# A hybrid encoder layer on one core: block sums taken by VectorE straight from the accumulator banks, and a later operand split issued directly behind its last product

## The chip, the core and the metric

The kernel runs on one core of a Trainium2 chip. The metric is device time in microseconds for one execution; the times before are 1273.06, 1273.35 and 1274.11 us, median 1273.35. The engines are TensorE (PE, with weight loads shown as PEld), VectorE (DVE), ScalarE (ACT), GpSimd (POOL) and SyncE (SP, which issues nearly all transfers). Each engine works through its own instructions in the order in which the program wrote them, and waits for semaphores where an operand or a buffer is not ready.

## What is computed

One layer on x of 1024 positions by 1024 channels, all in float32:

```
proj = x @ w_in + b_in                  # u | h | c_gate | b_gate | gate_a | gate_b
y_a  = S5 state space scan of u;  g = gelu(y_a)
y_a  = (g * sigmoid(g @ glu_w + glu_b)) @ w_ssm_out
y_b  = (b_gate * causal_conv(c_gate * h)) @ w_conv_out
mix  = (sigmoid(gate_a) * y_a + sigmoid(gate_b) * y_b) @ w_o
x    = layer_norm(ALPHA * x + mix)
ffn  = (silu(x @ w_gate) * (x @ w_up)) @ w_down
x    = layer_norm(ALPHA * x + ffn)
```

The gelu is the tanh form, 0.5 y (1 + tanh(c (y + 0.044715 y^3))). Below, v = b_gate * causal_conv(c_gate * h).

## The kernel before

**Tiling.** The three large products (input projection, gate and up projections of the FFN, down projection) use Strassen's seven products in place of eight. A `Pair` takes two column blocks of 128 weights; with the two halves of the inner dimension and the two halves of the 1024 positions this is a 2 by 2 block product, made of products 1 to 7 (`WOP` and `XOP` say which weight and operand blocks are added for each). A product is twelve matmuls of 128 x 512: every float32 operand is split into a rounded high part and a low remainder, and low x high, high x low and high x high are accumulated for four blocks of 128 (`Entry.mm`, L183 to L185). The high part is made by ScalarE, the low part by VectorE (`split` L120, `psplit` L131), the weight sums by GpSimd (`do_add`, L106 in `tt`).

**Sums of a pair.** The seven products of a pair go into four banks (`BANK_OF`): b0 takes products 2 then 4, b1 takes 5 then 3, b2 takes 1 then 7, b3 takes 6. b0 and b1 at their end are two of the four results. The other two need sums over banks, which `Pair.ev` issues after each product. Before the change: ScalarE copies b0 after product 2 (`ta`, L239), b1 after product 5 (`tb`, L242) and b2 after product 1 (`tc`, L245); GpSimd adds ta = ta + tb (L247, helper line L112) and tc = tc - ta (L250, helper line L115); VectorE then makes tb = b0 - ta (L265), tc = b1 + tc (L269), and adds b2 and b3 at the end (L271, L273). A bank may take its second product only when the first has been read out, and may go to another pair only when its last reader is done. Where one of the two GpSimd sums was issued in the same call, `wait` puts VectorE's part off to the call after the next product (`later`, `flush`).

**Order.** A program-wide list of steps, one per product, sets the order. At step s, `run` issues in turn: the weight sum of step s+4, the split of step s+3, one turn of every background generator (`bg`: the set-up of the scan, its eight chunks, the convolution, the gelu), the matmuls of s, what was put off, the step's `mid` functions and then `ev`. The input projection has 14 pairs, the FFN 22. In both, the first three pairs are interleaved, product by product (`LEAD_A`, `LEAD_D`; from here on the leads): 2, 4, 5, 3 for the three pairs in turn, then 1 and the rest. While they run, the operand blocks for the later products are still being made (`make_x`, `x1_rest`), and in the input projection the set-up of the scan runs on VectorE too. From the fourth pair on a pair's products follow one another: 2, 5, 1, 4, 3, 7, 6. The leads have six product banks between them; in the FFN the first two results of a pair stay in their banks until the gate is applied, and those of the third pair are copied out (`keep`, L256).

**v.** The conv branch's product with w_conv_out follows the input projection. Its operand v was written to memory and read back; `begin_b` splits it into vh and vl (eight pieces, ScalarE and VectorE), in place of the operands of the input projection. It was a `mid` function of the last step of the input projection, so behind that step's background turn and what was put off.

**gelu.** A background generator per tile of y_a: y is copied from its bank (L807), squared (L827), y (1/0.044715 + y^2) is made by VectorE (L830), ScalarE halves y in place (L831), then the tanh (L834) and the last product (L838).

Of the kernel before, what the change touches and what calls it, by code (L numbers as in the profile page):

```python
# [47 lines left out]
def kernel(  # L48
# [112 lines left out]
    class Step:  # L161
        load = add = split = mm = None

        def __init__(self):
            self.pre = []
            self.mid = []
            self.after = []

# [18 lines left out]
    class Pair:  # L187
        def __init__(self, s0, s1, nm, combos, epilogue):
# [4 lines left out]
            self.whole = {}  # L193
            self.done = set()
# [12 lines left out]
        def ev(self, m):  # L207
            d, e = self.done, self.evd
            d.add(m)
            fresh = set()  # L210

            def wait(name):
                if name in fresh:
                    later.append(lambda: self.ev(m))
                    fresh.discard(name)
                    fresh.add("-" + name)
                return "-" + name in fresh
# [22 lines left out]
            if once("cb", {5}):  # L240
                self.tb = tile("eb")
                S.activation(self.tb, self.b[1], AF.Copy)  # L242
            if once("cc", {1}):
                self.tc = tile("ec")
                S.activation(self.tc, self.b[2], AF.Copy)  # L245
            if once("s", {2, 5}):
                add(self.ta, self.ta, self.tb, G)  # L247
                fresh.add("s")
            if once("cs", {1}, "s"):
                sub(self.tc, self.tc, self.ta, G)  # L250
                fresh.add("cs")
# [10 lines left out]
            if 4 in d and "t11" not in e and wait("s"):  # L262
                pass
            elif once("t11", {4}, "s"):
                tt(self.tb, self.b[0], self.ta, ALU.subtract)  # L265
            if 3 in d and "t22" not in e and wait("cs"):
                pass
            elif once("t22", {3}, "cs"):
                add(self.tc, self.b[1], self.tc)  # L269
# [69 lines left out]

    def run(lo, hi):  # L340
        for s in range(lo, hi):
# [6 lines left out]
            for it in list(bg):  # L348
                if it[1] <= s:
                    try:  # L350
                        it[1] = s + max(1, next(it[0]) or 1)
                    except StopIteration:
                        bg.remove(it)
            steps[s].mm()
# [134 lines left out]
    for p in pairs[:3]:  # L489
        p.drops = {4: 1}  # L490
        p.whole = {2: wsum, 5: wsum}
    add_pairs(pairs, LEAD_A, 3)
# [272 lines left out]
    def flow(cc):  # L765
# [41 lines left out]
        S.activation(yn, ps, AF.Copy)  # L807
# [8 lines left out]
    def gelu(tl):  # L816
        yield 1
        for hs in ((0, 1),) if tl == 3 else ((0,), (1,)):
# [7 lines left out]
            for h in hs:  # L826
                S.activation(t[h], yf[h], AF.Square)  # L827
            yield 1
            for h in hs:
                V.scalar_tensor_tensor(t[h], t[h], 1.0 / 0.044715, yf[h], ALU.add, ALU.mult)  # L830
                S.activation(yf[h], yf[h], AF.Copy, scale=0.5)  # L831
            yield 2
            for h in hs:
                S.activation(t[h], t[h], AF.Tanh, scale=0.044715 * math.sqrt(2.0 / math.pi))  # L834
# [886 lines left out]
```

## Time and profile before

| | |
|---|---|
| median of three runs | 1273.35 us |
| the profiled execution, by its own time | 1274.3 us |
| span of the profile | 1272.5 us |
| PE busy | 1207.5 us (95% of the span) |
| DVE, ACT, POOL busy | 832.9, 764.7, 786.2 us |
| mean granted TensorE clock | 0.98 of full |

A row of a timeline gives the start, the time taken, engine, line, operation, output<-inputs, and in brackets the idle time before it and what ended that. Buffer numbers are left out of names. In names, the pair is the suffix: u (the pairs of u), hc (h with c_gate), b (b_gate), gt (gate_a with gate_b), f (FFN). `ps` is a product bank, `ea`, `eb`, `ec` are ta, tb, tc (in the second pair of a lead they are called `z`), `wh` and `wl` are high and low parts of weights, `xh`, `xl`, `x1h`, `x1l` those of operands, `hp` is a copy of the high part in a bank, `t` a weight sum, `xs` and `x1s` operand sums, `scr` the set-up of the scan.

### The profile page before, as it was taken

Reading aid. Unit: us, or ns where it says so; the run is one execution under the profiler, and the core shown is the slowest. Engines: PE = TensorE matmul, PEld = TensorE weight load, DVE = VectorE, ACT = ScalarE, POOL = GpSimd, SP = SyncE. Lnnn points to the kernel's source line nnn. Section 1 sums busy time; section 2 is a strip of 40 time slices with the busy share of each in tenths; the row PEclk is TensorE's granted clock in tenths of the full one; section 3 lists DMA queues with packets and bytes.
Section 4 is the critical chain, followed back from the end, with each engine's and each line's share of the span. In section 5 each row is a group of like instructions: output and inputs, shape, how many; then the busy total and the mean of one; then the engine's idle time right before and its main releaser. Section 6 shows DMA issues by size and latency. Waiting matters only on the chain. (4 is left out here: it accounts for less than half of the span.)

```text
span 1272.5 us, 16760 instructions
## 1 busy us (share of the span) xinstructions
PE 1207.5 (95%) x5341; PEld 977.6 (77%) x5341; DVE 832.9 (65%) x1338; ACT 764.7 (60%) x1360; POOL 786.2 (62%) x593
## 2 busy tenths in 40 slices
PE   7769999999899999999989999999999999999996
PEld 4547787787677888888867888888888887888776
DVE  6986887979665656688775444444444447667777
ACT  4676777696877333233674555554555655778891
POOL 4747787787762114323398787777787764544466
PEclk9989999999999999999989999999999999999998
DMA  7222334344447544324303522233223417937312
GB/s 262 67 68 92 86 123 119 112 130 137 136 141 228 193 158 163 113 87 143 139 34 116 181 101 108 94 113 116 98 93 108 153 71 267 370 100 214 101 47 87
DMA packets 88456, 167.63 MB, mean 132 GB/s; under 512 B 17841, under 2 KB 27057, under 8 KB 88113
## 3 DMA queue, kind: packets, MB, share of 16 engines
q1 hardware_dynamic: 87760, 166.44, 39.2%
q8 instruction: 42, 0.69, 0.2%
q14 instruction: 46, 0.37, 0.1%
q10 hardware_dynamic: 608, 0.13, 0.1%
HBM read 116.34 MB, written 44.83 MB: 127 GB/s over the span
## 5 line engine op out<-in xcount | busy, mean ns | idle before, releaser
L183 PE MATMUL ps_f<-x1h,wl_f 128*128 128x512 f32 x616 | 241.8, 393 | 6.0 <-ACT keep L256 2.3
L184 PE MATMUL ps_f<-x1l,wh_f 128*128 128x512 f32 x616 | 241.1, 391 | 1.9 <-DVE x1l L115 1.9
L185 PE MATMUL ps_f<-x1h,wh_f 128*128 128x512 f32 x616 | 240.9, 391 | 0.0
L115 DVE TENSOR_TENSOR wl_f<-t_f,hp 128x512 fp32r<-128x512 f32 x107 | 73.5, 687 | 167.9 <-ACT hp L137 167.5
L137 ACT ACTIVATE hp<-t_f 128x512 fp32r<-128x512 f32 x107 | 64.4, 601 | 163.6 <-POOL t_f L106 162.7
L183 PEld LDWEIGHTS ps_f<-x1h,wl_f 128*128 128x128 f32 x616 | 116.2, 189 | 32.2 <-ACT keep L256 2.8
L184 PEld LDWEIGHTS ps_f<-x1l,wh_f 128*128 128x128 f32 x616 | 116.5, 189 | 26.6 <-DVE x1l L115 2.3
L185 PEld LDWEIGHTS ps_f<-x1h,wh_f 128*128 128x128 f32 x616 | 116.4, 189 | 24.4
L106 POOL TENSOR_TENSOR tB<-B,B 128x512 f32<-128x512 f32 x55 | 71.2, 1294 | 85.1 <-DVE rBl L115 45.4
L1542 PE MATMUL pe<-rBh,rAl 128*128 128x512 f32 x297 | 116.1, 391 | 2.5 <-DVE acc L112 1.6
L1543 PE MATMUL pe<-rBl,rAh 128*128 128x512 f32 x297 | 115.8, 390 | 1.2 <-DVE rBl L115 1.2
L1544 PE MATMUL pe<-rBh,rAh 128*128 128x512 f32 x297 | 115.6, 389 | 0.0
L183 PE MATMUL ps_gt<-xh,wl_gt 128*128 128x512 f32 x216 | 88.9, 412 | 13.6 <-ACT ec_gt L245 3.7
L185 PE MATMUL ps_gt<-xh,wh_gt 128*128 128x512 f32 x216 | 87.1, 403 | 0.0
L184 PE MATMUL ps_gt<-xl,wh_gt 128*128 128x512 f32 x216 | 86.9, 403 | 0.0
L106 POOL TENSOR_TENSOR t_f<-raw_f,raw_f 128x512 f32<-128x512 f32 x63 | 81.8, 1300 | 2.2 <-DVE wl_f L115 2.0
L1542 PEld LDWEIGHTS pe<-rBh,rAl 128*128 128x128 f32 x297 | 55.8, 188 | 16.2 <-DVE acc L112 2.5
L1543 PEld LDWEIGHTS pe<-rBl,rAh 128*128 128x128 f32 x297 | 55.8, 188 | 13.3 <-DVE rBl L115 1.9
L138 ACT ACTIVATE wh_f<-t_f 128x512 fp32r<-128x512 f32 x107 | 66.0, 617 | 0.0
L1544 PEld LDWEIGHTS pe<-rBh,rAh 128*128 128x128 f32 x297 | 55.8, 188 | 11.6
L183 PEld LDWEIGHTS ps_gt<-xh,wl_gt 128*128 128x128 f32 x216 | 41.8, 194 | 26.6 <-ACT ec_gt L245 4.7
L109 POOL TENSOR_TENSOR hid<-sgf,ec_f 128x512 f32<-128x512 f32 x21 | 27.5, 1308 | 54.0 <-DVE sgf L109 29.1
(411 smaller groups left out, 3271.1 us busy)
## 6 DMA issues: line engine op xcount, KB each, us to landing
raw_f<-in_wgu SPq DMA_DIRECT2D x45, 512.0 KB, 4.0
As<-a_d SPq DMA_DIRECT2D x77, 256.0 KB, 3.9
a_d<-hs SPq DMA_DIRECT2D x55, 256.0 KB, 2.0
B<-in_wd SPq DMA_DIRECT2D x44, 256.0 KB, 5.4
s_d<-sg SPq DMA_DIRECT2D x32, 256.0 KB, 2.8
sgd<-s_d SPq DMA_DIRECT2D x16, 512.0 KB, 4.0
raw_gt<-in_w SPq DMA_DIRECT2D x15, 512.0 KB, 4.7
a_d<-hid SPq DMA_DIRECT2D x22, 256.0 KB, 2.1
```

Source lines behind the costliest of these rows:

```text
L106: eng.tensor_tensor(o, a, b, op)
L109: eng.tensor_tensor(o, a, b, ALU.mult)
L115: eng.tensor_tensor(o, a, b, ALU.subtract)
L137: S.activation(hp, raw, AF.Copy)
L138: S.activation(hi, raw, AF.Copy)
L183: PE.matmul(ps, self.lo[:, k, :], xh[:, k, :], start=first and k == 0, stop=False, skip_group_check=True)
L184: PE.matmul(ps, self.hi[:, k, :], xl[:, k, :], start=False, stop=False, skip_group_check=True)
L185: PE.matmul(ps, self.hi[:, k, :], xh[:, k, :], start=False, stop=last and k == 3, skip_group_check=True)
L1542: PE.matmul(ps, al[:, c], bh, start=kp == 0, stop=False)
L1543: PE.matmul(ps, ah[:, c], bl, start=False, stop=False)
L1544: PE.matmul(ps, ah[:, c], bh, start=False, stop=kp == NK - 1)
```

## The change

In `ev`, a pair that is `direct` keeps only the copy of b0. VectorE makes ta = b1 + ta from the bank behind product 5, and takes b2 and b1 straight into tc (x1 behind product 1, x3 behind product 3, whichever comes first starting tc by subtracting ta). `wait` is gone: nothing is put off but the two last epilogues. All 22 FFN pairs and the first three pairs of the input projection are direct. The eleven later pairs of the input projection keep the copies and the GpSimd sums. A pair that is `early` (the third of a lead) takes x3 only behind product 1. `begin_b` moves to directly behind the matmuls of the last step of the input projection, ahead of that step's background turn. In the gelu the factor 0.5 goes into the copy from the bank, with factors of 2 in the square and in the tanh to make up for it, and the halving goes.

```
-            if once("cb", {5}):
+            if not self.direct and once("cb", {5}):
                 self.tb = tile("eb")
                 S.activation(self.tb, self.b[1], AF.Copy)
-            if once("cc", {1}):
-                self.tc = tile("ec")
-                S.activation(self.tc, self.b[2], AF.Copy)
             if once("s", {2, 5}):
-                add(self.ta, self.ta, self.tb, G)
-                fresh.add("s")
-            if once("cs", {1}, "s"):
-                sub(self.tc, self.tc, self.ta, G)
-                fresh.add("cs")
+                if self.tb is None:
+                    tt(self.ta, self.b[1], self.ta, ALU.add)
+                else:
+                    add(self.ta, self.ta, self.tb, G)
+            banks = list(self.b)
...
-            if 4 in d and "t11" not in e and wait("s"):
-                pass
-            elif once("t11", {4}, "s"):
+            if once("t11", {4}, "s"):
+                if self.tb is None:
+                    self.tb = tile("eb")
                 tt(self.tb, self.b[0], self.ta, ALU.subtract)
-            if 3 in d and "t22" not in e and wait("cs"):
-                pass
-            elif once("t22", {3}, "cs"):
-                add(self.tc, self.b[1], self.tc)
+            for name, need, bk in (("x1", {1}, banks[2]), ("x3", {3}, banks[1])):
+                if (1 in d or not self.early) and once(name, need, "s"):
+                    if self.tc is None:
+                        self.tc = tile("ec")
+                        if self.direct:
+                            tt(self.tc, bk, self.ta, ALU.subtract)
+                        else:
+                            S.activation(self.tc, bk, AF.Copy)
+                            sub(self.tc, self.tc, self.ta, G)
+                    else:
+                        add(self.tc, bk, self.tc)
+            once("t22", set(), "x1", "x3")
...
+            if steps[s].next:
+                steps[s].mm()
+                steps[s].next()
+                advance(s)
+            else:
+                advance(s)
+                steps[s].mm()
...
+    for p in pairs[3:]:
+        p.direct = False
...
-        S.activation(yn, ps, AF.Copy)
+        S.activation(yn, ps, AF.Copy, scale=0.5)
...
-                S.activation(t[h], yf[h], AF.Square)
+                S.activation(t[h], yf[h], AF.Square, scale=2.0)
...
-                S.activation(yf[h], yf[h], AF.Copy, scale=0.5)
...
-                S.activation(t[h], t[h], AF.Tanh, scale=0.044715 * math.sqrt(2.0 / math.pi))
+                S.activation(t[h], t[h], AF.Tanh, scale=2.0 * 0.044715 * math.sqrt(2.0 / math.pi))
...
-    steps[n_co - 1].mid.append(begin_b)
+    steps[n_co - 1].next = begin_b
```

(`advance` is the loop over the background generators that stood in `run`.) In all, ScalarE loses 58 instructions (25 pairs by two copies, and eight halvings), GpSimd 50, VectorE gains 50. TensorE and SP keep their order unchanged. Three places show what moves.

The first is VectorE in the lead of the input projection, a piece of the difference, from about the third product of the first pair on (names ending in u and z_u are the first and second pair, gt the third).

```order
 L115 TENSOR_TENSOR xl_293<-xs_291,hp_346 128x512
+L106 TENSOR_TENSOR ea_u_196<-ps_u_1_337,ea_u_196 128x512
+L106 TENSOR_TENSOR eb_u_351<-ps_u_0_186,ea_u_196 128x512
 L115 TENSOR_TENSOR wl_u_3_356<-raw_u_0_198,hp_357 128x512
 L112 TENSOR_TENSOR scr<-scr 128x32 x3
 L118 TENSOR_SCALAR scr<-scr 128x32
 L115 TENSOR_TENSOR scr<-scr 128x32
-L106 TENSOR_TENSOR eb_u_350<-ps_u_0_186,ea_u_196 128x512
 L115 TENSOR_TENSOR xl_293<-xs_291,xh_292 128x512
```

The sum ta of the first pair is new on VectorE, and the subtraction behind it, which had been put off past the next split and three set-up rows, now stands directly behind it; both are ahead of the weights wl of the next product.

The second is ScalarE where the input projection ends: before,

```order
492 L121 ACTIVATE wh_so_1_0_3787<-raw_so_1_3679 128x512
493 L831 ACTIVATE gy_0_3715<-gy_0_3715 128x512
494 L831 ACTIVATE gy_1_3717<-gy_1_3717 128x512
495 L421 ACTIVATE sg_0_0_3821<-eb_gt_3704,b1s 128x512
496 L121 ACTIVATE vh<-vr_z 128x512
497 L121 ACTIVATE vh<-vr_ws 128x512
```

and now:

```order
480 L121 ACTIVATE wh_so_1_0_3775<-raw_so_1_3667 128x512
481 L121 ACTIVATE vh<-vr_z 128x512
482 L121 ACTIVATE vh<-vr_ws 128x512
483 L121 ACTIVATE vh<-vr_3549 128x512
484 L121 ACTIVATE vh<-vr_3575 128x512
```

Both halvings are gone from ahead of the first piece of vh, and the gate's sigmoid has moved behind the eighth. On VectorE nothing moves there.

The third is GpSimd in the lead of the FFN: before,

```order
237 L106 TENSOR_TENSOR x1s_0_5763<-M 128x512 x2
238 L112 TENSOR_TENSOR ea_f_5588<-ea_f_5588,eb_f_5772 128x512
239 L106 TENSOR_TENSOR x1s_2_5797<-M 128x512 x2
240 L112 TENSOR_TENSOR z_f_5613<-z_f_5613 128x512
241 L106 TENSOR_TENSOR t_f_1_5808<-raw_f_0_5394,raw_f_1_5639 128x512
242 L106 TENSOR_TENSOR x1s_0_5832<-M 128x512
243 L112 TENSOR_TENSOR ea_f_5637<-ea_f_5637,eb_f_5836 128x512
244 L106 TENSOR_TENSOR t_f_1_5839<-raw_f_0_5590,raw_f_1_5713 128x512
245 L106 TENSOR_TENSOR x1s_2_5865<-M 128x512
```

and now:

```order
231 L106 TENSOR_TENSOR x1s_0_5749<-M 128x512 x2
232 L106 TENSOR_TENSOR x1s_2_5782<-M 128x512 x2
233 L106 TENSOR_TENSOR t_f_1_5793<-raw_f_0_5380,raw_f_1_5625 128x512
234 L106 TENSOR_TENSOR x1s_0_5816<-M 128x512
235 L106 TENSOR_TENSOR t_f_1_5823<-raw_f_0_5576,raw_f_1_5699 128x512
236 L106 TENSOR_TENSOR x1s_2_5848<-M 128x512
```

The sums ta of the three pairs are gone from between the operand sums (x1s) and the weight sums (t). Three more go further on (the subtractions of tc, before at rows 251, 253 and 264).

More of the change, by code (lines that the diff above doesn't have):

```diff
@@ L167, in __init__ @@
             self.after = []
+            self.next = None
     class Entry:
@@ L193, in __init__ @@
             self.whole = {}
+            self.tb = self.tc = None
+            self.direct = True
             self.done = set()
@@ L209, in ev @@
             d.add(m)
[L210 to L217, printed above, removed]
             def once(name, need, *evs):
@@ L338, in flush, with advance @@
             f()
+    def advance(s):
+        for it in list(bg):
+            if it[1] <= s:
+                try:
+                    it[1] = s + max(1, next(it[0]) or 1)
+                except StopIteration:
+                    bg.remove(it)
     def run(lo, hi):
@@ L347, in run @@
                 steps[s + 3].split()
[L348 to L354, printed above, removed]
+            if steps[s].next:
[5 more added lines that the diff above has]
+                steps[s].mm()
             flush()
```

## The prediction

> **What bounds the kernel now.** I read the stages first, because the page's mean busy shares mix stages with different limits.
>
> ```profile
> core 0: us, PE busy (x) PEld busy (x) DVE busy (x) ACT busy (x) POOL busy (x), PEclk, DMA share, GB/s
> 46.00:100.00 54.00, 36.37 (x122) 27.16 (x121) 49.98 (x89) 35.42 (x62) 29.16 (x22) 0.82 0.18 54
> 100.00:405.00 305.00, 290.07 (x1381) 235.41 (x1381) 228.60 (x320) 225.38 (x383) 226.27 (x162) 0.99 0.43 132
> 405.00:412.00 7.00, 4.14 (x11) 2.75 (x10) 5.69 (x11) 6.17 (x12) 0.00 (x0) 0.76 0.44 130
> 646.00:696.00 50.00, 42.37 (x166) 32.79 (x166) 31.40 (x41) 28.98 (x54) 43.70 (x33) 0.93 0.20 72
> 696.00:1040.00 344.00, 344.00 (x1519) 284.82 (x1518) 149.47 (x234) 186.55 (x342) 262.48 (x210) 1.00 0.33 116
> ```
>
> Nineteen of the 22 FFN pairs lie in the last stretch, and there TensorE is busy for all of 344 us at full clock: 50 instructions moved from GpSimd to VectorE can win nothing there. What can be won lies in three holes: the lead of the input projection (46 to 100), the start of v's product (405 to 412) and the lead of the FFN (646 to 696). In the first VectorE is busy for 49.98 of 54 us, in the third GpSimd for 43.70 of 50. The same change takes GpSimd's load away and adds to VectorE's, so it should help in the third and may not in the first. TensorE's waits in these three stretches, in this order:
>
> ```profile
> PE ps_u L183 <- DVE ec_u L112: 6.0, 1, 6.0
> PE ps_u L183 <- DVE wl_u L115: 5.3, 3, 2.4
> PE ps_gt L183 <- ACT ec_gt L245: 3.3, 1, 3.3
> PE ps_gt L183 <- DVE wl_gt L115: 3.0, 1, 3.0
> ```
>
> ```profile
> PE pso L183 <- ACT vh L121: 2.9, 1, 2.9
> ```
>
> ```profile
> PE ps_f L183 <- ACT keep L256: 2.3, 1, 2.3
> PE ps_f L184 <- DVE x1l L115: 1.9, 1, 1.9
> PE ps_f L183 <- ACT ea_f L239: 1.7, 1, 1.7
> PE ps_f L183 <- DVE hid L109: 0.7, 1, 0.7
> PE ps_f L183 <- DVE eb_f L112: 0.7, 1, 0.7
> ```
>
> They are 17.6 us in the first hole, 2.9 in the second, 7.3 in the third. The granted clock adds to them: 0.82, 0.76 and 0.93 of full, since after each long idle stretch the matmuls ran at half clock for a while.
>
> **The price of the parts.** The instructions that go and the one that comes, by their groups:
>
> ```profile
> L242 ACT ACTIVATE eb_f<-ps_f 128x512 f32<-128x512 f32 x21 | 12.4, 593 | 9.0 <-PE ps_f L185 9.0
> L112 POOL TENSOR_TENSOR ea_f<-ea_f,eb_f 128x512 f32<-128x512 f32 x21 | 27.1, 1291 | 0.6 <-ACT eb_f L242 0.6
> L106 DVE TENSOR_TENSOR eb_f<-ps_f,ea_f 128x512 f32<-128x512 f32 x20 | 13.7, 684 | 0.2 <-POOL ea_f L112 0.2
> ```
>
> Per direct pair ScalarE loses two copies of 0.59 us, GpSimd two adds of 1.29, VectorE gains two sums of one bank and one SBUF operand, each 0.68 (0.60 from start to start in a row of them). Over 25 pairs: 30 us less ScalarE, 65 us less GpSimd, 30 to 34 us more VectorE. Off the path none of this counts; the path has four parts.
>
> **Input lead: 0 us.** VectorE has little idle time here, so what matters is how much work stands in its queue ahead of the last gate: product 7 of gt may go into its bank only when product 1 has been read out of it.
>
> ```profile
> 39.06 0.22 DVE L118 TENSOR_SCALAR scr<-scr 128x128 f32<-128x128 f32 x1
> 44.60 1.21 DVE L118 TENSOR_SCALAR scr<-scr 128x32 f32<-128x32 f32 x1
> 44.49 1.29 POOL L106 TENSOR_TENSOR t_u<-raw_u,raw_u 128x512 f32<-128x512 f32 x1
> 95.16 0.68 DVE L115 TENSOR_TENSOR xl<-xr,xh 128x512 fp32r<-128x512 f32 x1
> 95.33 0.79 PE L183 MATMUL ps_gt<-xh,wl_gt 128*128 128x512 f32 x1 [3.29 <-ACT ec_gt L245]
> ```
>
> Before, ScalarE's copy freed it for the start at 95.33. Now VectorE's x1 does, behind the xl that began at 95.16, with five new sums (three ta, two x1) ahead of it: 95.16 + 0.60 + 5 x 0.60 + 0.68 = 99.4, 4.1 us later. Against that stands what the missing GpSimd adds give back. A set-up row of 128x32 took 1.21 us where a larger one took 0.22: it ended at 45.81, just as GpSimd's instruction of 44.49 did (45.78). VectorE instructions that read SBUF alone were held to GpSimd's end; the new sums have a bank operand, and such rows are not. Each add that is gone can save one such wait, 1.0 us by these rows; five go ahead of this point, so 0 to 5 us. Walking the queue forward in the new order, I find about four of them saved, and x1 done within half a microsecond of 95.3. I take zero. The bounds are 4.1 later with nothing saved, and 3.8 earlier with all five saved and VectorE's own waits for ScalarE gone as well:
>
> ```profile
> DVE xl L115 <- ACT xh L121: 1.9, 2, 1.1
> DVE wl_u L115 <- ACT hp L137: 1.0, 2, 0.7
> ```
>
> (4.1 - 5 - 2.9 = -3.8.) Inside the lead the waits change places. The 6.0 us for ec_u go, because b1 of the first pair is read right behind its product 3; the wait ahead of the seventh product of gt grows from 3.3 to some 8 us.
>
> **gelu: -1 us.** Of the eight halvings in ScalarE's queue one was late for TensorE:
>
> ```profile
> 371.33 0.63 ACT L831 ACTIVATE gy<-gy 128x512 f32<-128x512 f32 x1 [0.98 <-ACT yn L807]
> 373.11 0.50 PE L183 MATMUL ps_gt<-xh,wl_gt 128*128 128x512 f32 x1 [0.89 <-ACT ea_gt L239]
> ```
>
> Behind it came a sigmoid and then the copy of b0 for which TensorE waited 0.89 us; without the halving and its wait of 0.98 this wait goes. The others are hidden behind TensorE's work, so 0 (spent again at the next wait) to 0.9, and I round up to 1 for a second halving ahead of a conv epilogue.
>
> **v: -2 us.** At the hand-over, ScalarE's queue, VectorE's and TensorE's second matmul (the first started as vh's first piece was done):
>
> ```profile
> 405.83 1.23 ACT L831 ACTIVATE gy<-gy 128x512 f32<-128x512 f32 x2 [1.57 <-DVE gl L830]
> 406.97 0.72 ACT L421 ACTIVATE sg<-eb_gt,b1s 128x512 f32<-128x512 f32 x1
> 407.60 0.61 ACT L121 ACTIVATE vh<-vr_z 128x512 fp32r<-128x512 f32 x1
> ```
>
> ```profile
> 406.25 0.68 DVE L112 TENSOR_TENSOR eb_gt<-ps_gt,eb_gt 128x512 f32<-128x512 f32 x1
> 408.24 0.69 DVE L115 TENSOR_TENSOR vl<-vr_z,vh 128x512 fp32r<-128x512 f32 x1 [1.31 <-ACT vh L121]
> 408.99 0.80 PE L184 MATMUL pso<-vl,wh_so 128*128 128x512 f32 x1
> ```
>
> With 2.9 us of waiting before a start at 408.2, the last product of the input projection ended at 405.4. ScalarE was idle then and goes straight to vh: 405.45 to 406.06. VectorE's order does not change, so the first vl comes behind eb_gt: 406.85 to 407.54, against 408.93 before. The second matmul starts 1.4 us earlier, and vl follows at 0.60 a piece, which is fast enough. The sigmoid and the tanh now come behind eight pieces of vh, some 4 us later; what reads them is a transfer and the gate's product much further on. On top comes the clock: at a mean of 0.76 over 7 us, 1.7 us were lost. Bounds 1.4 (clock as before) and 3.1 (clock full); I take 2.
>
> The Trainium skill, page "TensorE: Matmul & The Clock Gate", section "What's actually happening", says that TensorE falls to half clock after an idle window of about 3.4 us, on windows that run freely. By that rule this gap, cut to pieces of about 1 us, would leave the clock full, and the term would be 3.1, the sum 1.1 lower. The trace agrees as far as it goes (half clock after the 2.9 us here), but shows no gap of 1 us that begins inside a window, so I do not go by it.
>
> **FFN lead: -6 us.** GpSimd paces it, and the two longest waits go back to it.
>
> ```profile
> 646.93 1.76 DVE L106 TENSOR_TENSOR eb_f<-keep,ea_f 128x512 f32<-128x512 f32 x1 [1.66 <-POOL ea_f L112]
> 650.06 1.60 POOL L106 TENSOR_TENSOR x1s<-M 128x512 f32<-128x512 f32 x1 [1.92 <-DVE x1l L115]
> 656.00 0.58 ACT L256 ACTIVATE keep<-ps_f 128x512 f32<-128x512 f32 x1
> ```
>
> VectorE stood 1.66 us for GpSimd's ta and then 1.1 us more behind another of its instructions; the x1l that TensorE wanted came behind that, at 649.9. GpSimd's own next operand sum then waited 1.92 us for x1l, the weight sums came behind it, and ScalarE's keep, which frees the bank of the second pair's product 1, behind their splits. With ta on VectorE three adds of 1.29 us are gone from GpSimd ahead of this point. Walked forward, x1l is done near 648.0 and keep near 654.0, 2.6 us earlier than 656.58. Three more adds go behind it, 3 x 1.25 = 3.75, on the weight sums and FFN sums that lead to the wait for ea_f (1.7): 6.3 by the end. A new wait stands against it: product 3 of the third pair must now wait for ta in VectorE's queue, behind two splits, by up to one sum, 0.68. Most it could give is every wait and the lost clock, 7.3 + 0.07 x 50 = 10.8; least is the 2.6 less the new 0.7, so 2. I take 6.
>
> **FFN, later pairs: 0.** Here the new sums are covered, with this to spare:
>
> ```profile
> 809.58 0.69 DVE L115 TENSOR_TENSOR wl_f<-t_f,hp 128x512 fp32r<-128x512 f32 x1 [2.75 <-ACT hp L137]
> 810.00 0.58 ACT L245 ACTIVATE ec_f<-ps_f 128x512 f32<-128x512 f32 x1
> 811.87 0.39 PE L183 MATMUL ps_f<-x1h,wl_f 128*128 128x512 f32 x1
> ```
>
> Product 7 starts at 811.87 and needs b2 read out; the copy was done at 810.58. The new x1 stands behind that wl: 810.18 to 810.87, with 1.0 us left. If that cover went, each 1 us later would cost 19 us over the kernel.
>
> The Trainium skill, page "VectorE: DVE Perf Modes", gives a rule against this change: under "Rules for kernel authors", to copy a matmul's result to SBUF first if many operations follow, and, in the section on the TRN2 errata, 120 cycles of fixed cost from a bank against 58 from SBUF. By it I estimate 62 cycles at the page's 0.96 GHz, 0.065 us, per new sum, 0.3 us later in the input lead. The trace does not agree: the sum with a bank operand took 0.684 us, the xl at 95.16 with none 0.68.
>
> **Sum.** 0 - 1 - 2 - 6 = -9 us, on the profiled execution's 1274.3: 1265.3. That execution is 0.95 above the median of the runs, 1273.35, so the forecast there is 1264.4.
>
> **Rivals.**
> The input lead gains too, because VectorE's held rows shrink more than I count: TensorE waits for wl 5.3 us there, all in VectorE's queue, and VectorE's busy share of 93% speaks for it, the five added sums against it. At the bound, 3.8: 1260.6.
> The input lead loses: GpSimd's remaining sums are released by VectorE's splits and simply fall on other VectorE rows, so nothing is saved. 4.1 more: 1268.5.
> The FFN lead's waits only change their names: the first sums wait in VectorE's queue, and keep still waits behind the splits. GpSimd's 87% speaks against it. 2 in place of 6: 1268.4.
> Slower: in the later FFN pairs x1 (or ta, which product 3 now waits for) comes too late. It decides from 1.0 us of delay in VectorE's queue, where hid and sgf wait for GpSimd and ScalarE; one microsecond beyond costs 19: 1264.4 + 19 = 1283. GpSimd, lighter by 2.6 us a pair, feeds that queue earlier, which speaks against it.
> The move of v does not do what it says, because its first piece also waits for something that the profile does not show (the buffers that the last product reads, or the load): 1266.4.
>
> **Chances and range.** Forecast 0.50 (with its own range 1261 to 1268), input lead gaining 0.17, losing 0.14, FFN lead gaining little 0.10, v not earlier 0.04, slower 0.05. The range from 1258 to 1270 takes in all but the slower case and the ends of the others. A change below 0.2%, 2.5 us, cannot be told from none here. Only the cases that come together (input lead losing and FFN lead gaining little: 1264.4 + 4.1 + 4 = 1272.5) come out within that, so same 0.07; slower 0.04, a part of its case; faster 0.89.
>
> **What would show it.** Right: 50 fewer adds on GpSimd; no wait for ec_u; one wait of 7 to 9 us ahead of the last product of gt, on VectorE's ec_gt, with the product starting within 1 us of 95.3; vh starting within 0.2 us of the last matmul of the input projection, and TensorE's pause there cut by 1 us or more; no wait for x1l in the FFN lead, keep 2 to 3 us earlier; no new waits from 700 to 1030. Wrong: the product of gt starting before 92 or after 98; waits on ea_f or ec_f by VectorE in pair after pair of the FFN; a clock below 0.98 over the span.

## The result, and the profile after

The changed kernel took 1265.78 us (median of four runs, 1264.73 to 1267.08), the kernel before beside it 1273.73 (1273.06 to 1275.13): 0.9937 of the time, with a 95% interval of 0.9919 to 0.9954. Run once more later beside other kernels it took 1264.57 (1264.01 to 1266.91) against 1274.68: 0.9925, interval 0.9912 to 0.9938. So it is 8 to 10 us faster; forecast were 9 us and a median of 1264.4. The sum was right, but two of its four terms were not: the lead of the input projection lost 1 to 2 us where nothing was forecast, and the gelu gave nearly 3 us where 1 was forecast.

The stages of the changed kernel, in the columns of the prediction's first view:

```profile
46.00:100.00 54.00, 37.98 (x138) 28.32 (x139) 50.60 (x97) 36.51 (x63) 19.74 (x15) 0.85 0.18 54
100.00:405.00 305.00, 291.28 (x1389) 236.86 (x1387) 233.19 (x327) 225.54 (x384) 226.22 (x162) 0.99 0.44 134
405.00:412.00 7.00, 6.40 (x28) 5.28 (x29) 6.23 (x11) 4.34 (x8) 0.00 (x0) 1.00 0.24 77
646.00:696.00 50.00, 45.57 (x192) 36.61 (x191) 32.57 (x48) 30.40 (x55) 42.31 (x32) 0.97 0.36 127
696.00:1040.00 344.00, 344.00 (x1519) 284.93 (x1519) 174.93 (x274) 175.96 (x307) 212.44 (x168) 1.00 0.31 110
```

GpSimd lost 9.4 us of busy time in the first hole, and VectorE, with eight instructions more, gained 0.6. In the FFN's long stretch 50 us went from GpSimd and 25 came to VectorE, and TensorE is still busy for all of the 344 us. TensorE's waits in the three holes now (46 to 100, 402 to 412, 636 to 696):

```profile
PE ps_gt L184 <- DVE ec_gt L106: 9.3, 1, 9.3
PE ps_u L184 <- ACT hp L137: 7.4, 1, 7.4
PE ps_u L184 <- DVE wl_u L115: 5.8, 4, 3.0
```

```profile
PE pso L185 <- DVE vl L115: 1.8, 1, 1.8
```

```profile
PE ps_f L184 <- ACT keep L248: 3.5, 1, 3.5
PE ps_f L184 <- DVE ea_f L106: 1.5, 2, 0.9
```

The 6.0 us for ec_u are gone from the first hole, a wait of 7.4 is new, and the one ahead of gt's product 7 has grown from 3.3 to 9.3. In the FFN lead x1l, hid and eb_f have gone as reasons, and the wait for keep has grown from 2.3 to 3.5.

**Where the time went** is read best by following single matmuls. TensorE's order is the same in every kernel here, so a matmul of one trace can be set against the same matmul of another. The table gives how much later (+) or earlier (-) it started than in the profile of before, in us, each from its own span's start:

| matmul, with its start before | changed | changed, repeated | lead alone | gelu alone | v alone | FFN lead alone |
|---|---|---|---|---|---|---|
| first pair, product 3 (40.44) | +6.33 | +6.51 | +5.98 | -0.81 | -0.65 | -1.33 |
| first pair, product 1 (75.94) | -4.86 | -4.67 | -5.18 | -0.74 | -0.72 | -1.42 |
| gt, product 7 (95.33) | +2.21 | +2.39 | +1.87 | -0.76 | -1.78 | -2.50 |
| ahead of the first gelu copy (340.94) | +1.07 | +1.39 | +0.90 | -0.66 | +0.11 | -2.44 |
| behind the last (373.11) | -1.70 | -1.38 | +0.78 | -3.44 | -1.37 | -2.40 |
| end of the input projection (404.55) | -1.81 | -1.50 | +0.78 | -3.56 | -1.36 | -2.38 |
| v, ninth matmul and on (420.0) | -4.57 | -2.39 | +0.97 | -3.78 | -3.18 | -3.31 |
| ahead of the FFN lead (642.0) | -4.55 | -2.43 | +0.94 | -3.79 | -3.22 | -3.36 |
| behind it (700.0) | -9.29 | -7.17 | +0.94 | -3.78 | -3.19 | -8.40 |
| end of the FFN (1030) | -9.30 | -7.17 | +0.94 | -3.79 | -3.20 | -8.40 |
| last matmul (1262.08) | -9.18 | -7.46 | +1.39 | -3.62 | -3.43 | -8.09 |

A term is the difference between two rows of a column. The columns also show how much an execution differs from another where nothing was changed: with the gelu alone, v alone and the FFN lead alone the input lead is the old one, and yet gt's product 7 came 0.8, 1.8 and 2.5 us earlier than in the profile of before. A term read from one pair of traces is sure to about 2.5 us in the input lead, and to some tenths elsewhere, but for the clock. The profile of before is the latest of the executions with the old lead. Two kernels that follow, lead old (which has the old lead) and v early (the new one), add one execution each: product 7 starts at 92.8 to 95.3 in five executions with the old lead, 94.1 on the mean, and at 97.2 to 97.7 in four with the new one, 97.5 on the mean. So the new lead is 3.4 us late there by the means, and some 2 us late at 340.94.

### The profile page after: what moved, and what is told of

It reads as the page before. It is cut to its first block, busy times and chain, and to the rows that moved or that the text cites. A ratio compares the mean times of both kernels' runs of the same rounds, so it can differ in the third digit from the quotient of the medians.

```text
span 1263.3 us, 16654 instructions
## 1 busy us (share of the span) xinstructions
PE 1199.1 (95%) x5341; PEld 972.7 (77%) x5341; DVE 864.8 (68%) x1388; ACT 743.7 (59%) x1302; POOL 723.7 (57%) x543
## 5 line engine op out<-in xcount | busy, mean ns | idle before, releaser
L106 POOL TENSOR_TENSOR tB<-B,B 128x512 f32<-128x512 f32 x55 | 71.2, 1294 | 85.9 <-DVE rBl L115 45.4
L106 POOL TENSOR_TENSOR t_f<-raw_f,raw_f 128x512 f32<-128x512 f32 x63 | 83.2, 1321 | 11.6 <-DVE wl_f L115 11.6
L109 POOL TENSOR_TENSOR sgf<-sgf,eb_f 128x512 f32<-128x512 f32 x21 | 27.1, 1292 | 67.8 <-ACT sgf L1267 67.8
L106 POOL TENSOR_TENSOR t_f<-raw_f 128x512 f32<-128x512 f32 x43 | 57.2, 1332 | 11.9 <-DMA raw_f<-in_wgu 6.0
```

What stands on the lines that cost most here:

```text
L106: eng.tensor_tensor(o, a, b, op)
L109: eng.tensor_tensor(o, a, b, ALU.mult)
```

## One part at a time

Each of four kernels is the one before with one part of the change.

Lead alone: `Pair.direct` is false but for the first three pairs of the input projection, and `ev` of the kernel before serves all others.

```
+        def ev(self, m):
+            if not self.direct:
+                return self.ev_old(m)
...
     for p in pairs[:3]:
         p.drops = {4: 1}
         p.whole = {2: wsum, 5: wsum}
+        p.direct = True
```

> The kernel before, with only the three pairs of the input projection's lead made direct. The prediction: no change (0, between 3.8 less and 4.1 more), gt's product 7 within 1 us of 95.3. What the trace of the changed kernel suggests: 1.7 to 2.2 us more, gt's product 7 near 97.5, because the add that GpSimd no longer makes lets its operand and weight sums fall on other rows of VectorE. Rival: the lead is a gain, product 7 before 94, and what the changed kernel lost there comes from elsewhere.

Measured: 1275.38 us (1273.92 to 1278.23) against 1274.38, 1.0008 with an interval of 0.9999 to 1.0017, so 1 us more, though the interval just takes in no change. In its trace gt's product 7 started at 97.20, 1.87 us late, and not within 1 us of 95.3. The rival (a gain) fell; the prediction's zero fell by the trace, and by the time alone it cannot be ruled out. From there on the loss stood: 0.9 us of it were left at 341 and to the end of the FFN, 1.4 at the last matmul.

gelu alone: the factor 0.5 goes into the copy, the halvings go, and the square and the tanh get their factors of 2 (not shown here).

```
-        S.activation(yn, ps, AF.Copy)
+        S.activation(yn, ps, AF.Copy, scale=0.5)
...
-                S.activation(yf[h], yf[h], AF.Copy, scale=0.5)
```

> The kernel before, with only the factor 0.5 folded into the copy of y and the eight halvings gone. The prediction: 1 us less (0 to 0.9 by its bounds). What the trace suggests: about 3 us less, in three places between 340 and 375 us (waits for ea_gt, eb_gt, ea_gt of 0.9, 1.3 and 0.9 us that go, or shrink). Rival: the 3.4 us that TensorE made good between 100 and 375 us in the changed kernel belong to the lead (another phase of the clock and of GpSimd's sums); then this kernel gains 1 us or less.

Measured: 1271.24 us (1269.74 to 1273.21), 0.9975 (0.9965 to 0.9985), 3.1 us less. All of it comes between 341 and 373 us, in three steps of 1.2, 0.5 and 1.1, ahead of the matmuls at 348.64, 352.94 and 373.11. The rival, that the lead had moved the clock's phase, fell. What the prediction had overlooked is this, in the timeline of ScalarE before the change:

```profile
346.86 0.63 ACT L831 ACTIVATE gy<-gy 128x512 f32<-128x512 f32 x1 [1.09 <-DVE gl L830]
348.01 0.57 ACT L239 ACTIVATE ea_gt<-ps_gt 128x512 f32<-128x512 f32 x1
352.31 0.58 ACT L242 ACTIVATE eb_gt<-ps_gt 128x512 f32<-128x512 f32 x1
```

and in the changed kernel:

```profile
346.74 0.71 ACT L429 ACTIVATE sg<-ec_gt,b1s 128x512 f32<-128x512 f32 x1
347.35 0.58 ACT L234 ACTIVATE ea_gt<-ps_gt 128x512 f32<-128x512 f32 x1
```

A second halving, at 346.86, had waited 1.09 us for VectorE's gl, with a sigmoid and the copy of b0 behind it; TensorE waited 0.91 us for that copy, and then 1.27 for the next one, of which half goes too.

v alone:

```
-    steps[n_co - 1].mid.append(begin_b)
+    steps[n_co - 1].next = begin_b
```

> The kernel before, with only the split of v moved to directly behind the last product of the input projection. The prediction: 2 us less (1.4 to 3.1). What the trace suggests: 2.9 us less, the first matmul right behind the last product, the second waiting some 1.8 us for vl, and the clock full through the hand-over. Rival: the gain needs the gelu's halvings to be gone as well (they stood ahead of vh), then less than 1.4.

Measured: 1272.68 us (1270.24 to 1275.21), 0.9992 (0.9982 to 1.0003), 1.0 to 1.7 us less, not told apart from no change. In the trace the hand-over gave 1.8 us, of which 0.65 is the wait for vh (2.21 us, from 2.86) and the rest the clock (full here, half before). ScalarE in the timeline of this kernel, and then in that of the gelu alone:

```profile
404.45 1.23 ACT L840 ACTIVATE gy<-gy 128x512 f32<-128x512 f32 x2 [1.57 <-DVE gl L839]
405.59 0.61 ACT L121 ACTIVATE vh<-vr_z 128x512 fp32r<-128x512 f32 x1
```

```profile
403.26 0.72 ACT L421 ACTIVATE sg<-eb_gt,b1s 128x512 f32<-128x512 f32 x1 [2.76 <-DVE eb_gt L112]
403.88 0.61 ACT L121 ACTIVATE vh<-vr_z 128x512 fp32r<-128x512 f32 x1
```

Two things stood ahead of vh, halvings that wait for gl and a sigmoid that waits for eb_gt, each behind another row of the same VectorE queue. The gelu's part takes away the one, v's part the other; with both, in the changed kernel, vh started at 402.17, ahead of the input projection's last matmul at 403.19. The trace is on the rival's side, that the gain of v needs the halvings gone: without the clock v alone gave 0.65 us, less than 1.4. The times, 1.0 to 1.7 us, do not decide it.

FFN lead alone: as the lead alone, with `p.direct = True` for `fps[:3]` in place of `pairs[:3]`.

> The kernel before, with only the first three pairs of the FFN made direct, the other 19 as before. The prediction: 6 us less (2 to 10.8), all of the FFN's gain. What the trace suggests: 5 us less by the start of the fourth pair. Rival: the direct form of the 19 later pairs takes part (GpSimd lighter by 2.6 us a pair feeds the next weight sums), then this kernel gains 3 or less.

Measured: 1268.88 us (1266.16 to 1270.04), 0.9954 (0.994 to 0.9967), 5.5 us less. Its trace gives 5.0 us between 642 and 700, the changed kernel's 4.75 in both executions. So the three pairs are all of the FFN's gain, and the 19 later pairs give and cost nothing. The four parts make +1.0 - 3.1 - 1.7 - 5.5 = -9.3 us by medians, against 8.0 and 10.1 measured for the whole: within their noise they add up.

## Why the input lead lost: VectorE's rows beside GpSimd's

TensorE's new wait of 7.4 us ends at 46.8. The timeline of VectorE, GpSimd and TensorE there, changed kernel:

```profile
40.01 1.25 DVE L115 TENSOR_TENSOR scr<-scr 128x128 f32<-128x128 f32 x1
41.30 1.17 DVE L118 TENSOR_SCALAR scr<-scr 128x128 f32<-128x128 f32 x1
43.67 1.75 DVE L115 TENSOR_TENSOR xl<-xs,xh 128x512 fp32r<-128x512 f32 x1
45.94 0.68 DVE L106 TENSOR_TENSOR ea_u<-ps_u,ea_u 128x512 f32<-128x512 f32 x1
...
39.85 1.26 POOL L106 TENSOR_TENSOR t_u<-raw_u,raw_u 128x512 f32<-128x512 f32 x1
41.07 2.53 POOL L106 TENSOR_TENSOR xs<-xr,xr 128x512 f32<-128x512 f32 x2
...
46.77 0.76 PE L184 MATMUL ps_u<-xh,wl_u 128*128 128x512 f32 x1 [7.38 <-ACT hp L137]
```

Product 3 goes into the bank out of which VectorE takes ta, and ta was done at 46.62; the name in the bracket is of an instruction that ended 0.03 us later. ta is late because the set-up rows ahead of it took 1.0 to 1.25 us each. The prediction had quoted one of them at 0.22 us (at 39.06 before). Before, GpSimd stood still there and waited 2.75 us for ScalarE's copy of b1:

```profile
40.35 1.61 POOL L112 TENSOR_TENSOR ea_u<-ea_u,eb_u 128x512 f32<-128x512 f32 x1 [2.75 <-ACT eb_u L242]
```

Now it has no add to wait for, goes on with its operand and weight sums, and VectorE's rows run beside them.

The test puts a wait of that kind back without the add: one extra GpSimd instruction that reads ta.

```
                 if self.tb is None:
                     tt(self.ta, self.b[1], self.ta, ALU.add)
+                    if self.hold:          # the first pair
+                        self.hold = tile("ec")
+                        add(self.hold, self.ta, self.ta, G)
...
```

> The changed kernel, with one extra add on GpSimd (its result is not used) that reads the first pair's ta behind VectorE's sum, at the place in GpSimd's queue from which the add of ta went. It keeps GpSimd from its next operand and weight sums until VectorE has made ta, as in the kernel before. If VectorE's rows of 39 to 45 us are slow because those sums now run beside them, the four set-up rows of 128x128 take 0.2 to 0.3 us again in place of 1.0 to 1.25, ta is made near 42 in place of 46.6, and product 3 of the first pair starts near 42.2 in place of 46.8. Whether the end gains: by one theory nothing (VectorE's queue to gt's x1 is a sum of work, the sums fall on later rows instead, product 7 of gt stays within 1 us of 97.5); by the other the lead gains 2 us or more. Rival on the cause: the rows are slow for another reason, and stay at 1.0 or more.

The same three engines in the timeline of this kernel:

```profile
38.38 0.29 DVE L115 TENSOR_TENSOR scr<-scr 128x128 f32<-128x128 f32 x1
40.38 0.68 DVE L106 TENSOR_TENSOR ea_u<-ps_u,ea_u 128x512 f32<-128x512 f32 x1
42.30 3.63 DVE L112 TENSOR_TENSOR scr<-scr 128x32 f32<-128x32 f32 x3
...
41.14 1.04 POOL L112 TENSOR_TENSOR ec_u<-ea_u 128x512 f32<-128x512 f32 x1 [4.48 <-ACT hp L137]
...
98.04 0.80 PE L184 MATMUL ps_gt<-xh,wl_gt 128*128 128x512 f32 x1 [9.29 <-DVE ec_gt L106]
```

The set-up rows took 0.22 to 0.29 us, ta was done at 41.06 and product 3 started at 41.20, 5.6 us earlier; the rival, that the rows are slow for another reason, fell. Behind ta GpSimd's sums came all the same, and three rows of 128x32 that had taken 0.63 us together in the changed kernel took 3.63. gt's product 7 started at 98.04, 0.5 later, and the time was 1267.14 us (1265.93 to 1267.58). So the cause of the slow set-up rows is shown, and with it that VectorE is not saved from GpSimd's remaining sums by moving them: they fall on other rows.

Why x1 came 2.2 us late is the same once more, at the end of the lead. GpSimd, VectorE and TensorE in the timeline of the changed kernel:

```profile
94.35 1.65 POOL L106 TENSOR_TENSOR t_hc<-raw_hc,raw_hc 128x512 f32<-128x512 f32 x1 [3.57 <-DVE wl_hc L115]
...
94.91 1.37 DVE L112 TENSOR_TENSOR scr<-scr 128x256 f32<-128x256 f32 x1
96.20 0.68 DVE L115 TENSOR_TENSOR xl<-xr,xh 128x512 fp32r<-128x512 f32 x1
96.80 0.68 DVE L106 TENSOR_TENSOR ec_gt<-ps_gt,ea_gt 128x512 f32<-128x512 f32 x1
...
97.54 0.79 PE L184 MATMUL ps_gt<-xh,wl_gt 128*128 128x512 f32 x1 [9.33 <-DVE ec_gt L106]
```

Against the profile of before VectorE had no lag worth the name until 94.9 (0.09 us at the set-up row of 94.03 before), so in this pair all added sums had been paid for by then. Against the four other executions with the old lead they had not: the same row started at 91.53 to 93.28 in these, and at 93.79 to 94.30 in four with the new lead, a lag of 1.3 us on the mean of all. The weight sum t_hc, which before came at 96.95 behind the subtraction of tc, now falls on a set-up row that takes 1.37 us and took 0.42. That is 1 us; the rest is the split and x1 itself, which TensorE had not waited for before. Of VectorE's instructions that start from 39 to 100 us, take those that took over 0.15 us longer than the shortest of their operation and shape in these traces: there were 18 before with 17.3 us too much, and 15 in the changed kernel with 14.9. Over five executions with the old lead it is 16.0 to 17.3 us, over four with the new one 14.9 to 15.6. Six adds less in this stretch, five of them ahead of x1, saved 1.3 us of it on the mean and 2.5 in the first pair, not the four that the forecast rested on.

## What stands ahead of a row

Three more kernels take the changed one and alter an order or undo a part.

x1 first: `ev` of gt's product 1 directly behind its matmuls, ahead of the background turn.

```
+    steps[18].next = lambda: pairs[2].ev(1)
```

> The changed kernel, with x1 and x3 of gt issued directly behind the matmuls of gt's product 1, ahead of that step's background turn and operand piece (three set-up rows of 128x256 and one split). If the 9.3 us for which TensorE stands ahead of gt's product 7 are VectorE's queue, x1 is done near 94.8 in place of 97.5, product 7 starts 2.7 us earlier, and the end comes 2 to 3 us earlier (1263). Rival: TensorE only meets VectorE's queue at the next weights (wl of the fourth pair), and the end stays within 1 us.

x1 on VectorE in the timeline of this kernel:

```profile
93.29 0.68 DVE L106 TENSOR_TENSOR ec_gt<-ps_gt,ea_gt 128x512 f32<-128x512 f32 x1
```

Measured: 1262.72 us (1261.59 to 1266.82), 0.9917 (0.9901 to 0.9932); product 7 started at 94.03, 3.5 us earlier than in the changed kernel, and the last matmul 3.05 earlier. TensorE's wait was VectorE's queue, and the order in it is worth at least as much as the whole loss: 94.03 is where the old lead stands on the mean.

Lead old: the changed kernel with `ev` of the kernel before for the input projection; its eleven later pairs make the same sums in both forms, so this changes the three lead pairs.

> The changed kernel, with the three pairs of the input projection's lead back in the form of the kernel before (ScalarE's copies, GpSimd's sums); the other parts of the change stay. If the parts add up as they did alone (lead +1.0, gelu -3.1, v -1.7, FFN lead -5.5 by medians), 1 to 2 us less than the changed kernel: 1264 to 1265. Rival: the direct lead has a use that shows only with the others (ScalarE and GpSimd free earlier), then it is slower than the changed kernel.

Measured: 1263.06 us (1261.09 to 1265.05), 0.9912 (0.9897 to 0.9927). That is 1.5 to 2.7 us less than the two measurements of the changed kernel, as the sum of the parts says, though the intervals of the ratios overlap. In its profile product 7 came at 94.36, 3.2 us earlier; in that execution the hand-over to v, where the clock fell to half, took all of it back: the last matmul came at the same time as in the changed kernel.

v early: the sum eb_gt, the two rows of the gelu and their background turn go behind the eight pieces of v.

```
+    held, steps[n_co - 2].after = steps[n_co - 2].after, []
+    steps[n_co - 2].still = True           # no background turn at this step
-    steps[n_co - 1].next = begin_b
+    steps[n_co - 1].next = lambda: (begin_b(), [f() for f in held])
...
```

> The changed kernel, with what VectorE did between the last weights and the first vl (one sum of the last pair and two rows of the gelu, and the background turn they belong to) put behind the eight pieces of v. In the changed kernel the second matmul of v's product waited 1.8 us for the first vl, which stood behind these three rows. If that queue is all, the wait falls to 0.3 or less and the end comes 1.5 us earlier (1264). Rival: the gelu, now a step later, delays the gate's product, and the gain is given back (within 0.5 us or slower).

VectorE and TensorE in the timeline of the changed kernel, and then of this one:

```profile
404.26 0.69 DVE L112 TENSOR_TENSOR eb_gt<-ps_gt,eb_gt 128x512 f32<-128x512 f32 x1
404.86 0.68 DVE L115 TENSOR_TENSOR vl<-vr_z,vh 128x512 fp32r<-128x512 f32 x1
405.60 0.50 PE L185 MATMUL pso<-vl,wh_so 128*128 128x512 f32 x1 [1.79 <-DVE vl L115]
```

```profile
403.87 0.68 DVE L115 TENSOR_TENSOR vl<-vr_z,vh 128x512 fp32r<-128x512 f32 x1
404.60 0.51 PE L186 MATMUL pso<-vl,wh_so 128*128 128x512 f32 x1 [0.24 <-DVE vl L115]
```

Measured: 1262.43 us (1261.7 to 1263.74), 0.9908 (0.9895 to 0.9922); the wait fell to 0.24 and the last matmul came 1.5 us earlier than in the changed kernel. The intervals of these ratios overlap with those of the changed kernel, so the steps are read from the traces. Between 420 and 642 us TensorE gained and lost less than 0.1 us against the changed kernel's trace, so the later gelu cost nothing.

Then both orders together, and two kernels with x1 first in which gt alone goes back to ScalarE's copies and GpSimd's sums, beside the changed kernel:

```
-    for p in pairs[3:]:
+    for p in pairs[2:]:                    # "mix": gt is not direct
         p.direct = False
```

> The changed kernel itself once more, beside the three below on the same chip: 1265 to 1267, 0.992 to 0.995 of the kernel before.

> The changed kernel with both reorderings: x1 and x3 of gt directly behind its product 1, and v's eight pieces ahead of the three rows of VectorE. They lie 300 us apart; if they add up as they stood alone (3.1 and 3.4 us less by medians, 3 and 1.5 by the traces), 4.5 to 6 us less than the changed kernel: 1260 to 1261.5. Rival: what the first gains is given back by a wait for a load or at the gelu, so no more than 3 us less.

> The changed kernel with x1 and x3 of gt directly behind its product 1, and gt alone back to ScalarE's copies and GpSimd's sums (the first two pairs stay direct). ScalarE's copy frees the bank for product 7 ahead of VectorE's queue: by the theory that only this queue holds product 7, it starts at 92 or earlier in place of 94.0 in the kernel with x1 first, VectorE has two sums less, and the end is 1 to 3 us earlier than there (1260 to 1262). Rival: ScalarE's copy stands in its own queue behind instructions that wait for VectorE, and GpSimd's two sums hold other rows of VectorE, so no gain (within 1 us of 1262.7).

> The last kernel with v's eight pieces ahead of the three rows of VectorE as well: if all adds up, 1257 to 1260, the fastest here; by the rival, no faster than the kernel with both reorderings and a direct gt.

| kernel | median, us | runs | of the kernel before |
|---|---|---|---|
| changed, repeated | 1264.57 | 1264.01 to 1266.91 | 0.9925 (0.9912 to 0.9938) |
| x1 first and v early | 1262.33 | 1260.64 to 1263.67 | 0.9908 (0.9896 to 0.9921) |
| mix (x1 first, gt not direct) | 1265.07 | 1261.86 to 1266.3 | 0.9926 (0.9913 to 0.994) |
| mix and v early | 1261.94 | 1261.78 to 1262.15 | 0.9904 (0.9892 to 0.9917) |

The two orders did not add up: 2.2 us less, where 4.5 to 6 were expected. Against the trace of the changed kernel's repeat, product 7 came 2.7 us earlier, but 1.7 of these were gone when the input projection ended; the hand-over then gave 2.9, about half of that by the clock, and the last matmul came 3.3 us earlier. In the mix, product 7 started as early as forecast (timeline of TensorE):

```profile
91.86 0.50 PE L184 MATMUL ps_gt<-xh,wl_gt 128*128 128x512 f32 x1 [3.92 <-ACT ec_gt L265]
```

This is 5.9 us earlier than in the repeat of the changed kernel. By 142 us 3.5 of it were gone, at waits for ec_hc and cp of 0.8 to 1.4 us, most of which TensorE had not met when it came later, and the time shows none of the rest. The lead sets when the next stage starts, but not alone when it ends. The fastest kernel here by its median, mix with v early, is 12 to 13 us below the one before and 2.6 below the changed kernel beside it; the runs of these two do not overlap (the intervals of the two ratios just do). Whether it is faster than the kernel with both orders stays open.

## Why the prediction was right, and where not

**Input lead, forecast 0, measured +1.9 to +2.4 at product 7 by three traces, +0.9 to +1.4 at 340.94, and +1.0 by the runs of the lead alone.** The step that failed is "each add that is gone can save one such wait, 1.0 us by these rows ... I find about four of them saved". Price and bounds were right (x1 at 97.48 lies between the 99.4 with nothing saved and the far end), and so was the rule that VectorE's rows are held to GpSimd's end. But the walk took GpSimd's other sums to stay where they were. They moved up into the gaps that the adds had left and fell on other rows; 1.3 us were saved on the mean of the executions. This is the rival "the input lead loses", at a quarter to a half of its price of 4.1. The walk also started from one execution, the latest of the five with the old lead. Its second miss is the 7.4 us ahead of product 3, which needs ta: the forecast named that wait in the FFN lead and not here. It cost nothing, since VectorE's queue set the end of the lead. Right were the end of the wait for ec_u, and a long wait for ec_gt in its place (9.3 us, 7 to 9 forecast).

**gelu, forecast -1 (0 to 0.9), measured -2.8 in both traces and -3.1 by the runs.** The mechanism was right, the term mis-sized: one halving was counted (373.11, 1.1 us), two stood ahead of copies that TensorE waited for, and the other delayed two copies (1.7 us). "The others are hidden behind TensorE's work" was said without a row for it.

**v, forecast -2 (1.4 to 3.1), measured -2.8 in one execution and -0.9 in the other.** In the first the second matmul started 2.02 us behind the input projection's last product, against 3.59 before, so 1.6 us earlier (1.4 forecast), and vl set it, as said. The rest is the clock, which was full in the one execution and half in the other. What the forecast did not say is that its gain belongs to two edits together. The prediction also said that the trace of before shows no gap of 1 us that begins inside a window. It does: TensorE's gap of 1.27 us ahead of 352.94 lay in one window and left the clock full.

**FFN lead, forecast -6, measured -4.75 twice and -5.0 alone.** The wait for x1l is gone, as forecast, and with it those for hid and eb_f. keep came only 1.5 us earlier against the start of the lead (-4.55 to -6.08), where 2.6 was forecast, and TensorE's wait for it grew to 3.5. This is the part that was mis-sized, as the timeline shows:

```profile
643.88 1.62 POOL L106 TENSOR_TENSOR x1s<-M 128x512 f32<-128x512 f32 x1 [3.84 <-ACT wh_f L138]
645.45 3.04 POOL L106 TENSOR_TENSOR t_f<-raw_f,raw_f 128x512 f32<-128x512 f32 x2
...
647.29 0.60 ACT L137 ACTIVATE hp<-t_f 128x512 fp32r<-128x512 f32 x1 [2.39 <-POOL t_f L106]
...
650.54 0.64 PE L184 MATMUL ps_f<-x1h,wl_f 128*128 128x512 f32 x1 [3.54 <-ACT keep L248]
```

These are GpSimd, ScalarE and TensorE of the changed kernel: keep stands in ScalarE's queue behind a split that waits 2.39 us for a weight sum. The weight sum stands behind an operand sum ahead of which GpSimd itself had been idle for 3.84 us, by the profile until ScalarE's wh_f was done. So GpSimd no longer paces this place: relieved of the adds it waits for ScalarE, and "three adds of 1.29 us are gone" did not bring the weight sum forward by as much. On keep the rival was right ("keep still waits behind the splits"), on the whole it was not: behind keep, where the waits for hid, eb_f and ScalarE's ea_f went, 3.2 us came of 3.75 forecast. The new wait for ta was there (ea_f, 1.5 us in two, 0.7 forecast).

**FFN, later pairs, forecast 0, measured 0.** TensorE lost nothing, and the cover was larger than the 1.0 us of the forecast. The longest of VectorE's waits from 696 to 1035 us, before, and then some of them in the changed kernel:

```profile
DVE wl_f L115 <- ACT hp L137: 158.8, 80, 3.3
DVE hid L109 <- POOL sgf L109: 31.6, 18, 1.8
```

```profile
DVE hid L109 <- POOL sgf L109: 27.0, 18, 1.8
DVE ec_f L106 <- PE ps_f L186: 25.0, 18, 1.4
DVE wl_f L115 <- ACT hp L137: 24.0, 21, 1.3
DVE ea_f L106 <- PE ps_f L186: 16.4, 18, 0.9
```

With GpSimd lighter, the weights reach VectorE early, and x1 (ec_f, L106) now waits for TensorE's product and not behind a late wl. The rival that was slower needed the opposite. The prediction had named waits on ea_f or ec_f by VectorE in pair after pair as a sign of being wrong. They are there, 18 times each, and cost nothing, because VectorE waits for TensorE in them and not TensorE for VectorE: the sign was badly chosen.

**The sum.** It came out within 1.4 us, with +1 to +2, -2, -1 or +1 (by the clock) and +1 us of error in its terms: that they cancel is luck. The range, and that the change is faster, did not rest on it.

## To carry to other kernels

An engine relieved of work does not just finish earlier: it may wait for another one, and where it does not, its next instructions move up, and where they share something with another engine's they strike other rows there, so the saving is to be counted over the whole stretch and not by the rows that were struck before. On an engine whose queue sets the end of a stage, the place of the one row that frees a bank or feeds a product is worth as much as its number of rows; look at what the program issues between a product and the reading of its bank. Before a small instruction off the main chain is called hidden, look at every place where it occurs for a wait inside its own queue: it is the wait, not its 0.6 us, that is paid.

## What was not expected of the hardware

**The clock behind a short gap depends on where the gap falls.** At the hand-over to v, TensorE paused for 1.8 to 3.1 us in most of these kernels. The table has the gap ahead of the second matmul or, where the first waited, ahead of that one, the most idle time inside one window of 3.41 us (explained below), and what TensorE ran at behind the pause:

| gap, us | kernel | idle in one window, us | behind it |
|---|---|---|---|
| 0.24, 0.29, 0.46 | v early; mix and v early; both orders | 0.24, 0.30, 0.46 | full |
| 1.79 | changed | 1.18 | full |
| 1.90 | mix | 1.90 | half |
| 2.07 | changed, repeated | 2.07 | half |
| 2.15 | x1 first | 1.21 | full |
| 2.21 | v alone | 1.67 | full |
| 2.26, 2.26 | hold; lead old | 2.26, 2.91 | half |
| 2.70, 2.85, 2.86 | gelu alone; lead alone; before | 2.45, 2.85, 2.73 | half |
| 3.09 | FFN lead alone | 1.93 | full |

Two rows of TensorE's timeline from the mix, and two from the FFN lead alone:

```profile
403.02 0.61 PE L185 MATMUL pso<-vl,wh_so 128*128 128x512 f32 x1 [1.90 <-DVE vl L115]
403.42 0.63 PE L186 MATMUL pso<-vh,wh_so 128*128 128x512 f32 x1
```

```profile
406.11 0.50 PE L183 MATMUL pso<-vh,wl_so 128*128 128x512 f32 x1 [3.09 <-ACT vh L121]
407.18 0.40 PE L185 MATMUL pso<-vh,wh_so 128*128 128x512 f32 x1
```

A matmul in a row of them takes 0.39 to 0.40 us at full clock and 0.63 at half. The same kernel met both in two executions, and this alone is most of the 2 us between its two columns at 420 us.

The length of the gap does not sort the table; the third column nearly does. In each of the 14 traces all grants of half clock start whole multiples of 3.41 us apart, so the time is cut into windows of that length, which lie differently in each execution. Of the windows at full clock between 30 and 1255 us, the 4777 with less than 1.6 us of TensorE's idle time in them were all followed by full clock, the 77 with 1.95 or more all by half clock, and of the 44 in between 11 were followed by half. The gap of 3.09 us was shared by two windows, 1.93 us in the first. For a kernel with such a gap the clock is therefore a draw, since the place of the windows is not in its hands; a gap under 1.6 us was safe here wherever it fell, unless another stood in the same window.

The rule of the Trainium skill that the prediction had named (page "TensorE: Matmul & The Clock Gate", section "What's actually happening") has the windows right, which run freely. Its idle window of about 3.4 us does not fit: 1.90 us of idle time in a window was enough, and the 2.86 us before, which the prediction took for agreement, were less than such a window too. The term that the prediction had worked out by it, 3.1 us, was nearly met in one execution (2.8) and missed in the other (0.9).

**Held rows wait for GpSimd's end.** The rows of VectorE that were held from 39 to 100 us are of two SBUF operands and, as at 41.30 in the changed kernel, of one (1.17 us, where the same shape took 0.22 at 39.06 before). The Trainium skill, page "SBUF — State Buffer", section "SBUF: two separate sides", tells of a pair of ports that VectorE and GpSimd share and that one instruction holds for its whole length; the trace agrees, as the held rows got through only when GpSimd's instruction was done (GpSimd's of 94.35 ended at 96.00, VectorE's of 94.91 at 96.28). This was so row after row before and after the change: held rows of 128x32 ended 0.04 to 0.05 us behind the end of a GpSimd instruction, those of 128x256 0.28, those of 128x512 0.55, whatever they had taken in all; a row that was only slowed would not keep such a distance. None of the rows with a bank operand was held. What the runs add is that the held time is nearly kept when GpSimd's work moves: 17.3 us before, 14.9 in the changed kernel, 17.1 with the extra add.
